# One pool for all raw tiles, tied places for the rest of the rows, and score steps and transposes at other places, in a hybrid decoder layer

## The chip, the cores and the metric

The kernel runs on one core of one Trainium2 chip. The metric is the device time of one execution in microseconds. The kernel before takes 1724.84 us, the median of three runs (1724.03 to 1726.55). The execution that the profiler recorded took 1727.64 us.

## The reference

One layer on 4096 rows of 1024 float32 values:

```python
proj = x @ w_in                      # 1024 x 2832, cut into q_a, k_a, v_a, g_a | q_b, k_b, v_b, g_b, r_b
q_a, k_a = partial_rope(q_a), partial_rope(k_a)          # 8 query heads, 2 key heads of 64, first 16 dims
out_a = softmax(window 128, with a sink per head)(q_a, k_a) @ v_a * silu(g_a)
log_a = log_sigmoid(r_b @ w_up + b_gate) / 16
o_b   = gla_chunked(q_b / 8, k_b, v_b, log_a)            # 4 heads, chunks of 64, a state carried over the chunks
out_b = o_b * rsqrt(mean(o_b ** 2) + 1e-5) * norm_w * silu(g_b)
out   = layer_norm(2 ** 0.25 * x + concat(out_a, out_b) @ w_out, ln_g, ln_b)
```

## The kernel before

The rows are worked in 32 blocks of 128 (`NB` = 32). There are three stages, each a loop over all blocks: A is the windowed attention, B the gated linear attention, C the output projection with the layer norm. A and B leave their branch in HBM (`mixd`), and C loads it again.

Every large product is made of three float32r products: a tensor is cut into a high part (a cast) and a low part (the tensor less its high part), and high x high, high x low and low x high are added up. So each loaded ("raw") tile of 128x512 float32 is cast once and subtracted once. For the rows of a block these are two tiles, q = 0 (k = 0 to 3) and q = 1 (k = 4 to 7). GpSimd casts them (L103) and VectorE subtracts (L106). Both parts go to `xq`, which has four places in stage A; the rows of block n+2 take the place of block n-2. For weights, ScalarE casts and VectorE or GpSimd subtracts.

Block n of stage A is issued in this order (L488 to L537):

- The rows of block n+2 are fetched (`fetch_x`, two DMAs on SyncE's queue).
- The query projection `pq` runs over k = 0 to 7 with three matmuls of 512 columns for each k. After every second k one step of the generator `a_scores` of block n-1 is taken. The four steps make the scores `psc` of two heads each. The first two belong to head group g = 0, the other two to g = 1. After each, VectorE masks the scores and takes the maximum. After steps two and four come ScalarE's exponentials and VectorE's normalisation (`pr`, L414).
- `pkv`, the key and value projection, follows; VectorE applies the rotation (L315 to L320).
- `pg`, the gate projection, is done "turned" for the pair of blocks (n, n+1 for even n), 6 matmuls of 256 columns for each k; an even n makes columns 0 and 1 of the pair, an odd n columns 2 and 3. So the places of a pair of rows come free in the odd block: k = 0 to 3 first, k = 4 to 7 at the end of its `pg`.
- Between parts of `pg` run the steps of `a_out` of block n-1: `turn(0)` and `turn(1)` (transposes `pt`, cut into `hl` by ScalarE and VectorE, then four masked copies `p` each by GpSimd's affine select, L439), `mul(0)` and `mul(1)` (four matmuls `po` each, L454, and VectorE's `att`). Then there are the transposes of the keys (`a_turn_k`) and of the queries (`a_turn_q`: `tq`, cut into `qs`, VectorE's parts at L351 for heads 0 to 3 of the first half and L353 for the second).
- Last come the gate (`a_gate`, VectorE's part `sg` at L364) and the generator of this block's scores.

Blocks 0 and 30 project the queries of two blocks, and blocks 1 and 31 of none.

The order on each engine is not exactly this. A planner places each instruction by its own estimate of when its inputs and buffers are ready, and prefers what is earlier in the program. Work whose inputs and buffers are free early is moved ahead, across blocks too. On the chip each engine and each DMA queue then works strictly in the planned order. `after(ins, earlier)` adds an edge that only fixes the order.

Raw tiles lie in these pools before: `xw` (two buffers) for rows in A and B and for `mixd` tiles in C; `wr` (three buffers in A, another three in B and C) for weights loaded after the start. Weights of B are loaded in A's blocks 2, 30 and 31, those of C in B's last block.

Of the kernel before, what the change touches and what calls it, by code (L numbers as in the profile page):

```python
# [9 lines left out]
F32 = mybir.dt.float32  # L10
F32R = mybir.dt.float32r
# [3 lines left out]
ALU = mybir.AluOpType  # L15
# [4 lines left out]
P = 128  # L20
# [30 lines left out]
def layer_kernel(  # L51
# [18 lines left out]
    NB = xt.shape[0]  # L70
# [4 lines left out]
    xp = ctx.enter_context(tc.tile_pool(name="xp", bufs=1))  # L75
    xw = ctx.enter_context(tc.tile_pool(name="xw", bufs=2))
    ps = ctx.enter_context(tc.tile_pool(name="ps", bufs=2, space=PSUM))
# [37 lines left out]

    def load_group(wr, src, c0, n, slot, width, early=False):
        hs, ls = [], []
        for k in range(NK):
            raw = wr.tile([P, 512], F32, tag="wraw", name=f"wraw{slot}_{k}")
            sp.dma_start(raw[:, :n], src[k, :, c0 : c0 + n])  # L120
            h = wp.tile([P, width], F32R, tag=f"wh{slot}_{k}", name=f"wh{slot}_{k}")
            l = wp.tile([P, width], F32R, tag=f"wl{slot}_{k}", name=f"wl{slot}_{k}")
            split(h[:, :n], l[:, :n], raw[:, :n], act, dve if early or k % 2 == 0 else pool)
            hs.append(h)
            ls.append(l)
        return hs, ls

    def load_halves(wr, src, c0, slot):

        hs, ls = ([wp.tile([P, 512], F32R, tag=f"w{t}{slot}_{k}", name=f"w{t}{slot}_{k}") for k in range(NK)] for t in "hl")  # L130
        for i in range(2):
            c = slice(256 * i, 256 * i + 256)
            for k in range(0, NK, 2):
                raw = wr.tile([P, 512], F32, tag="wraw", name=f"wraw{slot}_{k}_{i}")
# [26 lines left out]
    def load_x(n, heng, leng, places):  # L161
        for x in split_x(n, fetch_x(n), heng, leng, places):
            pass
        return x

# [22 lines left out]
    with ExitStack() as pa:  # L188
        e1 = pa.enter_context(tc.tile_pool(name="e1", bufs=1))
        wr = pa.enter_context(tc.tile_pool(name="wra", bufs=3))  # L190
        with ExitStack() as pstart:
# [11 lines left out]
            raws, xs = [], []  # L203
# [93 lines left out]
        vvs = {-1: v0}  # L297
        tanh = [None]

# [39 lines left out]
        def a_turn_q(n, qk):  # L339

            tq = bank("tp", f"tq{n}")
            for j in range(4):
                pe.transpose(
                    tq[:, j * P : (j + 1) * P],
                    qk[:, 2 * j : 2 * j + 2, :].rearrange("p h d -> p (h d)"),
                    ident,
                )
            qs = e1.tile([P, 8, P], F32R, tag="qs", name=f"qs{n}")
            tqv = tq.rearrange("p (j s) -> p j s", j=4)
            act.copy(qs[:64, :4, :], tqv[:64])  # L350
            dve.tensor_tensor(qs[64:, :4, :], tqv[:64], qs[:64, :4, :], ALU.subtract)  # L351
            act.copy(qs[:64, 4:, :], tqv[64:])
            dve.tensor_tensor(qs[64:, 4:, :], tqv[64:], qs[:64, 4:, :], ALU.subtract)  # L353
            return qs
# [63 lines left out]
        def a_out(n, pn):  # L418
# [4 lines left out]
            parts = {}  # L423

            def turn(g):
# [7 lines left out]
                act.copy(hr, ptv)  # L433
                dve.tensor_tensor(hl[:, 1].bitcast(F32R), ptv, hr, ALU.subtract)
                for i in range(2):
# [51 lines left out]
        for n in range(NB):  # L487
            last = n == NB - 1  # L488
            raws = fetch_x(n + 2) if 0 < n < NB - 2 else None
            both = n in (0, NB - 2)  # L490
            group = [n, n + 1] if both else [] if n in (1, NB - 1) else [n]
            pqs = [bank("pj", f"pq{m}") for m in group]
            for i in range(4):
                for m, pq in zip(group, pqs):
                    project(pq, xs[m], wq, 512, 2 * i, 2 * i + 2)
                if scores:
                    pn = next(scores)
            for m, pq in zip(group, pqs):
                qks[m] = a_q(m, pq)
            if n == NB - 2:  # L500
                wb["v"] = load_group(wr, w_b, 528, 512, 0, 512)
            for m in group:
# [3 lines left out]
            if n == 0:  # L506
                wg = load_halves(wr, w_a, 768, 2)
                raws = fetch_x(2)
            if n == NB - 2:
                wb["q"] = load_group(wr, w_b, 0, 272, 1, 272)  # L510
            if n == 2:
                wb["k"] = load_group(wr, w_b, 272, 256, 3, 256)
# [12 lines left out]
            project_turned(pg, xpair, wg, cols, 6, 7)  # L525
            qs = a_turn_q(n, qks[n])
            xs.extend(parts)
            project_turned(pg, xpair, wg, cols, 7, 8)
            next(po, None)
            if last:  # L530
                bx_next = load_x(0, pool, dve, 2)
                wb["g"] = load_group(wr, w_b, 1040, 512, 2, 512)
            a_gate(n, pg)
# [15 lines left out]
    with ExitStack() as pb:  # L549
        wr = pb.enter_context(tc.tile_pool(name="wrb", bufs=3))  # L550
        f1 = pb.enter_context(tc.tile_pool(name="f1", bufs=1))
# [230 lines left out]
        for n in range(NB):  # L782
            x, last = bx_next, n == NB - 1
            if not last:
                bx_next = load_x(n + 1, pool, dve, 2)
            pq = bank("pj", f"bq{n}")
# [19 lines left out]
            if last:  # L806
                wo[0] = load_group(wr, w_o, 0, 512, 0, 512)
            pk = bank("pj", f"bk{n}")
# [11 lines left out]
            if last:  # L820
                wo[1] = load_group(wr, w_o, 512, 512, 2, 512)
        b_attn(NB - 1)
# [6 lines left out]
    with ExitStack() as pcx:  # L829
# [126 lines left out]
```

## Time and profile before

| | us |
|---|---|
| median of 3 runs | 1724.84 |
| profiled execution | 1727.64 |
| its span, first to last instruction | 1725.9 |
| stage A, about | 0 to 672 |
| stage B, about | 672 to 1372 |
| stage C, about | 1372 to the end |

The span covers all but 1.74 us of the profiled execution. In the rows below a time in front of a line is the start from the span's beginning, the number behind it the duration, and a bracket at the end is idle time of that engine before the instruction with what ended it. Matmuls overlap their neighbours in these rows: one of 512 columns is shown some 0.39 us long and the next starts 0.23 us after it; one of 256 columns is shown 0.28 us long and the next starts 0.12 us after it. A row of a stretch gives its limits, its length, the busy us (and the number of instructions) of PE, PEld, DVE, ACT and POOL, the mean granted clock of TensorE, the busy share of the DMA engines, and GB/s.

### The profile page before, as it was taken

What the parts mean: (1) busy time and instruction counts of PE and PEld (TensorE: products, weight loads), DVE (VectorE), ACT (ScalarE), POOL (GpSimd) and SP (SyncE); (2) the same over time, 40 slices, a digit from 0 to 9 for tenths busy, and PEclk for the clock granted to TensorE, in tenths of its full rate; (3) what the DMA queues carried; (4) which work ended last, traced back from release to release, by engine and by line L of the source; (5) the groups of instructions that cost most, each with busy time, mean ns of one, the idle gap of its engine ahead of it and who ended that gap; (6) DMA issues with size and microseconds to landing.
All of it is one profiled execution on the core that took longest, in us unless ns stands there. A gap on an engine that the chain in (4) does not pass through costs nothing.

```text
span 1725.9 us, 27803 instructions
## 1 busy us (share of the span) xinstructions
PE 1684.8 (98%) x10117; PEld 1482.6 (86%) x10117; DVE 1130.8 (66%) x2602; ACT 785.4 (46%) x2110; POOL 504.6 (29%) x623
## 2 busy tenths in 40 slices
PE   8999999999999999999999999999999899999998
PEld 8788888888888887888888888888888788888886
DVE  7777777777777776666666666666666755555554
ACT  6544434444443455555555555555555622222221
POOL 1433333233333345222222222222222422222221
PEclk9999999999999999999999999999999999999999
DMA  6211111111111132111111111111111544444442
GB/s 189 83 37 43 43 41 49 42 37 38 38 38 44 37 100 80 33 38 39 39 40 38 38 38 38 38 38 38 37 38 38 172 158 143 143 143 146 147 135 86
DMA packets 76478, 119.80 MB, mean 69 GB/s; under 512 B 23858, under 2 KB 30388, under 8 KB 76340
## 3 DMA queue, kind: packets, MB, share of 16 engines
q1 hardware_dynamic: 76340, 118.02, 21.4%
q8 instruction: 80, 1.31, 0.3%
q14 instruction: 58, 0.48, 0.1%
HBM read 84.37 MB, written 33.62 MB: 68 GB/s over the span
## 4 chain that ended last, share of the span: by engine, by line
PE 83%; DVE 8%; POOL 3%; issue 3%; ACT 3%; DMA 1%; DVEq 0%; POOLq 0%; ACTq 0%; SPq 0%
PE py L173 7%; PE py L172 7%; PE py L171 7%; PE bv L173 3%; PE bg L171 3%; PE bv L172 3%; PE bv L171 3%; PE bg L173 3%; PE bg L172 3%; PE pg L185 3%; PE pg L183 3%; PE pg L184 3%; PE po L454 2%; PE psc L389 2%; PE pq L173 2%
## 5 line engine op out<-in xcount | busy, mean ns | idle before, releaser
L439 POOL TENSOR_SCALAR_AFFINE_SELECT p<-hl 128x512 fp32r<-128x512 f32 x256 | 170.3, 698 | 335.0 <-ACT hl L433 302.0
L103 POOL TENSOR_SCALAR xq<-xraw 128x512 fp32r<-128x512 f32 x124 | 77.8, 632 | 429.9 <-issue 303.1
L171 PE MATMUL py<-wh,xq 128*128 128x512 f32 x512 | 200.2, 391 | 0.0
L173 PE MATMUL py<-wh,xq 128*128 128x512 f32 x512 | 200.2, 391 | 0.0
L172 PE MATMUL py<-wl,xq 128*128 128x512 f32 x512 | 200.0, 391 | 0.0
L408 ACT ACTIVATE pr<-psc,ngm 128x128 f32<-128x128 f32 x256 | 90.7, 367 | 158.7 <-DVE ngm L403 147.1
L183 PE MATMUL pg<-xq,wh 128*128 128x256 f32 x512 | 154.7, 302 | 3.0 <-DVE vv L325 1.7
L871 POOL TENSOR_TENSOR y<-y,lg 128x1024 f32<-128x1024 f32 x31 | 74.1, 2392 | 267.2 <-ACT y L870 267.2
L185 PE MATMUL pg<-xq,wl 128*128 128x256 f32 x512 | 145.5, 284 | 0.3 <-DVE wl L106 0.3
L184 PE MATMUL pg<-xq,wh 128*128 128x256 f32 x512 | 145.2, 284 | 0.0
L106 DVE TENSOR_TENSOR xq<-xraw,xq 128x512 fp32r<-128x512 f32 (+1 forms) x132 | 111.4, 844 | 45.2 <-POOL xq L103 40.8
L172 PEld LDWEIGHTS py<-wl,xq 128*128 128x128 f32 x512 | 96.7, 189 | 20.2
L171 PEld LDWEIGHTS py<-wh,xq 128*128 128x128 f32 x512 | 96.7, 189 | 20.0
L173 PEld LDWEIGHTS py<-wh,xq 128*128 128x128 f32 x512 | 96.5, 189 | 19.9
L171 PE MATMUL bg<-wh,xq 128*128 128x512 f32 x256 | 106.2, 415 | 0.0
L101 ACT CAST xq<-mr 128x512 fp32r<-128x512 f32 x64 | 39.6, 622 | 140.2 <-PE py L172 135.1
L171 PE MATMUL bv<-wh,xq 128*128 128x512 f32 x256 | 103.2, 403 | 0.0
L171 PE MATMUL pq<-wh,xq 128*128 128x512 f32 x256 | 100.1, 392 | 1.6 <-DVE sg L364 1.6
L854 DVE SCALAR_TENSOR_TENSOR y<-xr,py 128x512 f32<-128x512 f32 x64 | 44.0, 687 | 87.8 <-PE py L173 87.7
L183 PEld LDWEIGHTS pg<-xq,wh 128*128 128x128 f32 x512 | 98.3, 192 | 3.5 <-DVE vv L325 1.9
L173 PE MATMUL pq<-wh,xq 128*128 128x512 f32 x256 | 101.1, 395 | 0.0
L172 PE MATMUL pq<-wl,xq 128*128 128x512 f32 x256 | 100.8, 394 | 0.0
(220 smaller groups left out, 5027.2 us busy)
## 6 DMA issues: line engine op xcount, KB each, us to landing
xraw<-in_xt_dram SPq DMA_DIRECT2D x124, 256.0 KB, 2.7
mr<-mx SPq DMA_DIRECT2D x64, 256.0 KB, 3.0
xr<-in_xn_dram SPq DMA_DIRECT2D x32, 512.0 KB, 3.6
out_dram<-y SPq DMA_DIRECT2D x31, 512.0 KB, 2.6
mx<-att SPq DMA_DIRECT2D x32, 256.0 KB, 2.7
mx<-mb SPq DMA_DIRECT2D x32, 256.0 KB, 2.0
wraw<-in_w_b_dram SPq DMA_DIRECT2D x16, 256.0 KB, 3.0
wraw<-in_w_o_dram SPq DMA_DIRECT2D x16, 256.0 KB, 3.2
```

The costliest lines, as they stand in the source:

```text
L103: pool.tensor_scalar(hdst, src, 1.0, 1.0, ALU.mult, ALU.mult)
L106: leng.tensor_tensor(ldst, src, hdst, ALU.subtract)
L171: pe.matmul(dst[:, :n], a, hs[k][:, :n], start=(k == 0), stop=False)
L172: pe.matmul(dst[:, :n], a, ls[k][:, :n], start=False, stop=False)
L173: pe.matmul(dst[:, :n], b, hs[k][:, :n], start=False, stop=(k == NK - 1))
L183: pe.matmul(o, hs[k][:, c], a, start=(k == 0 and i == 0), stop=False)
L184: pe.matmul(o, hs[k][:, c], b, start=False, stop=False)
L185: pe.matmul(o, ls[k][:, c], a, start=False, stop=(k == NK - 1 and i == 1))
L408: act.activation(pr[:, i], sc[i], AF.Exp, bias=ngm[:, h : h + 1], scale=0.125, accum_out=den[:, h : h + 1])
L439: pool.affine_select(o, hl[:, i], [[0, 4], [sg_, P]], ALU.is_gt if b else ALU.is_ge, 0.0, base=0, channel_multiplier=-sg_,)
L854: dve.scalar_tensor_tensor(y[:, s], xr[:, s], ALPHA, py, ALU.mult, ALU.add)
L871: pool.tensor_tensor(y, y, lg, ALU.mult)
```

## The change

All raw tiles (rows, weights, and the tiles of C) come from one pool `xw` with six buffers under one tag; the pools `wr` are gone. `fetch_x` with GpSimd issues a row tile's cast right behind its load. The subtraction (`rest_x`) is a call of its own. In stage A the subtraction of q = 0 is tied behind the last `hl` subtraction on VectorE and that of q = 1 behind the last `qs` subtraction (L353); in the order of the program the casts stand at the head of the block. The four score steps stand after k = 3, 5, 7 and 8 of `pq` (before: 2, 4, 6, 8). `turn(0)` stands after the first k of `pg` (before: ahead of it); `turn(1)` and all later steps keep their places. In stage B `load_x` does cast, cast, subtract, subtract (before: cast, subtract, cast, subtract).

```diff
-    xw = ctx.enter_context(tc.tile_pool(name="xw", bufs=2))
+    xw = ctx.enter_context(tc.tile_pool(name="xw", bufs=6))
...
-            raw = wr.tile([P, 512], F32, tag="wraw", name=f"wraw{slot}_{k}")
+            raw = xw.tile([P, 512], F32, tag="raw", name=f"wraw{slot}_{k}")
...
-    def fetch_x(n):
+    def fetch_x(n, heng, places=4):
+
         raws = []
         for q in range(2):
-            raws.append(xw.tile([P, 4, P], F32, tag="xraw", name=f"xraw{n}_{q}"))
-            sp.dma_start(raws[q], xt[n][:, 4 * q : 4 * q + 4])
+            s = slice(4 * q, 4 * q + 4)
+            raws.append(xw.tile([P, 512], F32, tag="raw", name=f"xraw{n}_{q}").rearrange("p (k s) -> p k s", k=4))
+            sp.dma_start(raws[q], xt[n][:, s])
+            if heng is pool:
+                pool.tensor_scalar(rows_of(n, places)[0][:, s], raws[q], 1.0, 1.0, ALU.mult, ALU.mult)
         return raws
 
-    def split_x(n, raws, heng, leng, places=4):
+    def rest_x(n, raws, q, places=4):
+
         h, l = rows_of(n, places)
+        s = slice(4 * q, 4 * q + 4)
+        return dve.tensor_tensor(l[:, s], raws[q], h[:, s], ALU.subtract)
+
+    def load_x(n, places):
+        raws = fetch_x(n, pool, places)
         for q in range(2):
-            s = slice(4 * q, 4 * q + 4)
-            split(h[:, s], l[:, s], raws[q], heng, leng)
-            yield h, l
...
+            rest_x(n, raws, q, places)
+        return rows_of(n, places)
...
-            raws = fetch_x(n + 2) if 0 < n < NB - 2 else None
+            raws = fetch_x(n + 2, pool) if 0 < n < NB - 2 else None
...
-                    project(pq, xs[m], wq, 512, 2 * i, 2 * i + 2)
+                    project(pq, xs[m], wq, 512, (0, 3, 5, 7)[i], (3, 5, 7, 8)[i])
...
-            next(po, None)
-            parts = split_x(n + 2, raws, pool, dve) if raws else iter(())
...
-            project_turned(pg, xpair, wg, cols, 0, 3)
+            project_turned(pg, xpair, wg, cols, 0, 1)
+            next(po, None)
+            project_turned(pg, xpair, wg, cols, 1, 3)
             next(po, None)
             project_turned(pg, xpair, wg, cols, 3, 6)
             next(po, None)
-            next(parts, None)
+            if raws:
+                ins = rest_x(n + 2, raws, 0)
+                if n > 0:
+                    after(ins.ins, hl_last[0].ins)
             a_turn_k(n, kks[n])
             project_turned(pg, xpair, wg, cols, 6, 7)
             qs = a_turn_q(n, qks[n])
-            xs.extend(parts)
+            if raws:
+                after(rest_x(n + 2, raws, 1).ins, qs_last[0].ins)
+                xs.append(rows_of(n + 2))
             project_turned(pg, xpair, wg, cols, 7, 8)
...
-                raws.append(xw.tile([P, 4, P], F32, tag="xraw", name=f"mr{n}_{q}"))
+                raws.append(xw.tile([P, 512], F32, tag="raw", name=f"mr{n}_{q}").rearrange("p (k s) -> p k s", k=4))
```

## Rows read from the trace of the kernel before

**Rows 1.** The page's busy times by engine.

```profile
PE 1684.8 (98%) x10117; PEld 1482.6 (86%) x10117; DVE 1130.8 (66%) x2602; ACT 785.4 (46%) x2110; POOL 504.6 (29%) x623
```

**Rows 2.** TensorE's waits, 81 to 616 us: total, times, longest.

```profile
PE psc L389 <- DVE qs L351: 11.1, 13, 1.4
PE pt L429 <- DVE es L404: 1.6, 7, 0.3
```

**Rows 3.** Busy times by stretch: block 5, block 6 of A; then most of B.

```profile
112.63:132.00 19.37, 19.37 (x135) 17.95 (x134) 13.61 (x33) 8.57 (x29) 6.32 (x10) 1.00 0.08 28
132.00:152.78 20.78, 19.95 (x135) 17.84 (x134) 15.93 (x38) 8.43 (x30) 6.63 (x11) 1.00 0.16 52
...
721.00:1340.00 619.00, 619.00 (x3862) 550.33 (x3861) 385.86 (x896) 342.75 (x840) 168.76 (x200) 1.00 0.13 38
```

**Rows 4.** TensorE's timeline: starts of blocks 4 and 29, and block 5's end.

```profile
91.81 0.39 PE L171 MATMUL pq<-wh,xq 128*128 128x512 f32 x1
...
125.48 0.60 PE L429 MATMUL pt<-cs,pr 128*128 128x128 f32 x4
...
128.07 1.09 PE L454 MATMUL po<-p,vv 128*128 128x512 f32 x4
...
131.08 1.09 PE L454 MATMUL po<-p,vv 128*128 128x512 f32 x4
...
134.31 0.74 PE L389 MATMUL psc<-kd,qs 128*128 128x256 f32 x4 [0.76 <-DVE qs L351]
...
596.17 0.39 PE L171 MATMUL pq<-wh,xq 128*128 128x512 f32 x1
```

**Rows 5.** VectorE's timeline in blocks 5 and 6.

```profile
123.61 0.69 DVE L414 TENSOR_TENSOR pr<-pr,rec 128x512 f32<-128x512 f32 x1
...
125.87 0.68 DVE L434 TENSOR_TENSOR hl<-pt,hl 128x512 fp32r<-128x512 f32 x1
...
128.47 0.69 DVE L106 TENSOR_TENSOR xq<-xraw,xq 128x512 fp32r<-128x512 f32 x1 [0.99 <-POOL xq L103]
129.86 0.68 DVE L463 TENSOR_TENSOR att<-po,tmp 64x512 f32<-64x512 f32 x1 [0.70 <-ACT tmp L462]
...
132.46 1.08 DVE L106 TENSOR_TENSOR xq<-xraw,xq 128x512 fp32r<-128x512 f32 x1 [1.58 <-POOL xq L103]
133.57 0.69 DVE L351 TENSOR_TENSOR qs<-tq,qs 64x512 fp32r<-64x512 f32 x1
```

**Rows 6.** GpSimd's timeline in block 5.

```profile
126.62 1.23 POOL L439 TENSOR_SCALAR_AFFINE_SELECT p<-hl 128x512 fp32r<-128x512 f32 x2 [0.91 <-DVE hl L434]
127.82 0.62 POOL L103 TENSOR_SCALAR xq<-xraw 128x512 fp32r<-128x512 f32 x1
128.59 1.07 POOL L439 TENSOR_SCALAR_AFFINE_SELECT p<-hl 128x512 fp32r<-128x512 f32 x1 [0.16 <-PE po L454]
...
131.80 1.20 POOL L103 TENSOR_SCALAR xq<-xraw 128x512 fp32r<-128x512 f32 x2 [0.38 <-DMA xraw<-in_xt_dram]
```

**Rows 7.** The start: TensorE's and GpSimd's timelines, then one stretch of 5 us.

```profile
49.18 0.63 PE L429 MATMUL pt<-cs,pr 128*128 128x128 f32 x4 [1.76 <-DVE pr L414]
...
46.67 1.83 POOL L103 TENSOR_SCALAR xq<-xraw 128x512 fp32r<-128x512 f32 x2 [4.24 <-DMA xraw<-in_xt_dram]
...
50.00:55.00 5.00, 4.15 (x14) 3.17 (x14) 3.51 (x7) 1.70 (x4) 5.00 (x8) 0.66 0.31 83
```

**Rows 8.** From A to B: TensorE's and VectorE's timelines, then one stretch.

```profile
618.67 0.50 PE L171 MATMUL pq<-wh,xq 128*128 128x512 f32 x1 [1.58 <-DVE sg L364]
...
616.09 1.08 DVE L106 TENSOR_TENSOR xq<-xraw,xq 128x512 fp32r<-128x512 f32 x1 [1.69 <-POOL xq L103]
...
665.00:670.00 5.00, 5.00 (x18) 4.20 (x18) 2.02 (x4) 2.42 (x5) 2.91 (x5) 0.55 0.18 50
```

**Rows 9.** From B to C: TensorE's timeline, then one stretch.

```profile
1368.16 0.66 PE L742 MATMUL bo<-bvv,al 128*128 128x128 f32 x4 [1.58 <-DVE al L106]
...
1370.00:1375.00 5.00, 4.61 (x14) 3.71 (x14) 2.74 (x7) 1.99 (x4) 2.36 (x3) 0.50 0.85 284
```

More of the change, by code (lines that the diff above doesn't have):

```diff
@@ L114, in load_chunk, with load_group @@
         return h, l, raw
-    def load_group(wr, src, c0, n, slot, width, early=False):
+    def load_group(src, c0, n, slot, width, early=False):
         hs, ls = [], []
         for k in range(NK):
-            raw = wr.tile([P, 512], F32, tag="wraw", name=f"wraw{slot}_{k}")
+            raw = xw.tile([P, 512], F32, tag="raw", name=f"wraw{slot}_{k}")
             sp.dma_start(raw[:, :n], src[k, :, c0 : c0 + n])
@@ L126, in load_group, with load_halves @@
         return hs, ls
-    def load_halves(wr, src, c0, slot):
+    def load_halves(src, c0, slot):
         hs, ls = ([wp.tile([P, 512], F32R, tag=f"w{t}{slot}_{k}", name=f"w{t}{slot}_{k}") for k in range(NK)] for t in "hl")
@@ L133, in load_halves @@
             for k in range(0, NK, 2):
-                raw = wr.tile([P, 512], F32, tag="wraw", name=f"wraw{slot}_{k}_{i}")
+                raw = xw.tile([P, 512], F32, tag="raw", name=f"wraw{slot}_{k}_{i}")
                 for j in range(2):
@@ L145, in rows_of @@
         return xq[:, n % places, 0], xq[:, n % places, 1]
-    def fetch_x(n):
+    def fetch_x(n, heng, places=4):
         raws = []
         for q in range(2):
-            raws.append(xw.tile([P, 4, P], F32, tag="xraw", name=f"xraw{n}_{q}"))
-            sp.dma_start(raws[q], xt[n][:, 4 * q : 4 * q + 4])
+            s = slice(4 * q, 4 * q + 4)
[3 more added lines that the diff above has]
+                pool.tensor_scalar(rows_of(n, places)[0][:, s], raws[q], 1.0, 1.0, ALU.mult, ALU.mult)
         return raws
-    def split_x(n, raws, heng, leng, places=4):
+    def rest_x(n, raws, q, places=4):
         h, l = rows_of(n, places)
+        s = slice(4 * q, 4 * q + 4)
+        return dve.tensor_tensor(l[:, s], raws[q], h[:, s], ALU.subtract)
+    def load_x(n, places):
+        raws = fetch_x(n, pool, places)
         for q in range(2):
-            s = slice(4 * q, 4 * q + 4)
-            split(h[:, s], l[:, s], raws[q], heng, leng)
-            yield h, l
[L161 to L164, printed above, removed]
+            rest_x(n, raws, q, places)
+        return rows_of(n, places)
     def project(dst, x, wg, n, k0=0, k1=NK):
@@ L189, in layer_kernel @@
         e1 = pa.enter_context(tc.tile_pool(name="e1", bufs=1))
-        wr = pa.enter_context(tc.tile_pool(name="wra", bufs=3))
         with ExitStack() as pstart:
@@ L297, in layer_kernel @@
         vvs = {-1: v0}
-        tanh = [None]
+        tanh, hl_last, qs_last = [None], [None], [None]
         def swapped(n):
@@ L352, in a_turn_q @@
             act.copy(qs[:64, 4:, :], tqv[64:])
-            dve.tensor_tensor(qs[64:, 4:, :], tqv[64:], qs[:64, 4:, :], ALU.subtract)
+            qs_last[0] = dve.tensor_tensor(qs[64:, 4:, :], tqv[64:], qs[:64, 4:, :], ALU.subtract)
             return qs
@@ L433, in turn @@
                 act.copy(hr, ptv)
-                dve.tensor_tensor(hl[:, 1].bitcast(F32R), ptv, hr, ALU.subtract)
+                hl_last[0] = dve.tensor_tensor(hl[:, 1].bitcast(F32R), ptv, hr, ALU.subtract)
                 for i in range(2):
@@ L500, in layer_kernel @@
             if n == NB - 2:
-                wb["v"] = load_group(wr, w_b, 528, 512, 0, 512)
+                wb["v"] = load_group(w_b, 528, 512, 0, 512)
             for m in group:
@@ L506, in layer_kernel @@
             if n == 0:
-                wg = load_halves(wr, w_a, 768, 2)
-                raws = fetch_x(2)
+                wg = load_halves(w_a, 768, 2)
+                raws = fetch_x(2, pool)
             if n == NB - 2:
-                wb["q"] = load_group(wr, w_b, 0, 272, 1, 272)
+                wb["q"] = load_group(w_b, 0, 272, 1, 272)
             if n == 2:
-                wb["k"] = load_group(wr, w_b, 272, 256, 3, 256)
+                wb["k"] = load_group(w_b, 272, 256, 3, 256)
             po = a_out(n - 1, pn) if n > 0 else iter(())
             pg = bank("pj", f"pg{n}")
-            next(po, None)
-            parts = split_x(n + 2, raws, pool, dve) if raws else iter(())
             cols = (0, 1) if n % 2 == 0 else (2, 3)
             xpair = xq[:, n // 2 % 2 * 2 : n // 2 % 2 * 2 + 2]
-            project_turned(pg, xpair, wg, cols, 0, 3)
+            project_turned(pg, xpair, wg, cols, 0, 1)
+            next(po, None)
+            project_turned(pg, xpair, wg, cols, 1, 3)
             next(po, None)
@@ L530, in layer_kernel @@
             if last:
-                bx_next = load_x(0, pool, dve, 2)
-                wb["g"] = load_group(wr, w_b, 1040, 512, 2, 512)
+                bx_next = load_x(0, 2)
+                wb["g"] = load_group(w_b, 1040, 512, 2, 512)
             a_gate(n, pg)
@@ L549, in layer_kernel @@
     with ExitStack() as pb:
-        wr = pb.enter_context(tc.tile_pool(name="wrb", bufs=3))
         f1 = pb.enter_context(tc.tile_pool(name="f1", bufs=1))
@@ L784, in layer_kernel @@
             if not last:
-                bx_next = load_x(n + 1, pool, dve, 2)
+                bx_next = load_x(n + 1, 2)
             pq = bank("pj", f"bq{n}")
@@ L806, in layer_kernel @@
             if last:
-                wo[0] = load_group(wr, w_o, 0, 512, 0, 512)
+                wo[0] = load_group(w_o, 0, 512, 0, 512)
             pk = bank("pj", f"bk{n}")
@@ L820, in layer_kernel @@
             if last:
-                wo[1] = load_group(wr, w_o, 512, 512, 2, 512)
+                wo[1] = load_group(w_o, 512, 512, 2, 512)
         b_attn(NB - 1)
```

## The prediction

> **What bounds the kernel now.** I read the page's busy times first. TensorE is busy 1684.8 us of a span of 1725.9 us, VectorE 1130.8 us [rows 1]. So TensorE sets the time and only what makes it wait can be won. Next I asked what TensorE waits for between 81 and 616 us, where stage A runs evenly: 11.1 us in 13 waits for VectorE's `qs` at the first score step, 1.6 us for `es` [rows 2]. Thirteen in 26 blocks means every second block, so I set two neighbours beside each other. Block 5 takes 19.37 us with TensorE busy throughout, block 6 takes 20.78 us, though both do the same 135 matmuls (pieces counted in the row) [rows 3]. The 1.41 us between them is more than the 0.76 us of idle time that the timeline shows before `psc` [rows 4]. The idle time is too small a measure: a matmul's shown end reaches past the start of its successor, so some 0.16 us of each wait (0.39 less 0.23) is shown as busy, and the late block has smaller delays behind the first. So I count block lengths. Block 4 starts at 91.81 us and block 29 at 596.17 us [rows 4]: 504.36 us for 13 even and 12 odd blocks. Taking 19.37 us for each odd one leaves 271.9 us, or 20.92 us for an even one. The excess is 1.55 us each and 20.1 us in all.
>
> The Trainium skill speaks of this under "Performance Expectations" in "Trainium Kernel Development and Optimization": matmul busy time is a bad metric since matmuls are pipelined, and the weight loads' busy share is a good one. The first half agrees with the 0.76 against 1.41 us. By the second half block 5 would have 1.42 us to spare too (17.95 busy of 19.37 us [rows 3]), an estimate from that page's rule; I take none of it, for nothing in block 5 waits.
>
> Why is the even block late? Its VectorE timeline [rows 5] shows the subtraction of a row tile at 132.46 us, after 1.58 us of idle time for GpSimd's cast, 1.08 us long, and right behind it, at 133.57 us, the `qs` part that the scores need. GpSimd's cast ran at 131.80 us, when the place in `xq` came free at the end of the odd block's `pg` [rows 6]. VectorE works in order, so `qs`, gate and `att` stand behind that subtraction. In stage B TensorE is busy 619.00 of 619.00 us [rows 3].
>
> **The change part by part.** *The ties.* The subtraction of q = 0 now follows the last `hl`, that of q = 1 follows L353. Neither can stand ahead of L351 with its cast late: the q = 0 cast has its place free when k = 3 of the odd block's `pg` is done. Without that subtraction `qs` (L351) can start when its inputs are there, some 2 us earlier. The subtractions themselves are not saved; q = 0 falls into VectorE's gap between the last `hl` (done about 127.5 us) and `att` (129.86 us) [rows 5], q = 1 into the wait for the first scores. If that second cover is gone, it costs what it pushes the softmax. The two bounds of one q = 1 subtraction are 0.69 and 1.08 us [rows 5].
>
> *The score steps.* The first step comes 9 instead of 6 matmuls into `pq`: 3 x 0.23 = 0.70 us later, and the second and third likewise; the fourth stays. This alone would hide 0.70 of the mean 0.85 us wait (11.1 / 13). Its price is that `pr` of g = 1 comes later. In block 5 it ends at 124.30 us and `pt` of g = 1 starts at 125.48 us [rows 4, 5]: a margin of 1.2 us, of which I see 0.7 us used. With a pushed q = 1 subtraction it could all be used; then `pt` is late by up to 0.6 us.
>
> *`turn(0)` one k later.* It moves 6 x 0.12 = 0.72 us. GpSimd's second pair of copies waits for VectorE's `hl` (125.87 us), which stands behind the rotation and not behind `pt` [rows 5, 6]. So `mul(0)` at 128.07 us should not move: the pair ends at 127.85 us, and the fourth matmul of `mul(0)` starts at 128.07 + 3 x 0.23 = 128.76 us, a margin of 0.9 us of which the later `hl` takes about 0.65.
>
> *Casts and six buffers.* Both blocks' rows can now be in SBUF when the places come free, so two q = 0 casts may go into the gap in which before one fits (127.82 to 128.59 us). In block 5 the copies for `mul(1)` end at 131.43 us (131.80 less the 0.38 us of idle), and its fourth matmul starts at 131.08 + 0.69 = 131.77 us [rows 4, 6]: margin 0.34 us. A second cast of 0.62 us costs 0 to 0.3 us. I take 0.2 us in each pair of blocks, the value nearest to these rows.
>
> *Sum for the even part.* 13 x (1.55 - 0.2) = 17.5 us won. Bounds: 20.1 us won, and 16 us lost if `pt` is late by 0.6 us in all 26 blocks and nothing is won.
>
> *The start.* At 46.67 us GpSimd waited 4.24 us for a row tile's load, which had to wait for one of two buffers; VectorE stood behind that cast and TensorE 1.76 us behind VectorE; from 50 to 55 us the granted clock was 0.66, that is, part of the stretch at the lower level, which costs 0.34 x 5 = 1.7 us [rows 7]. Six buffers load sooner, and the tie takes the subtraction out of the way; but block 2's weights now share the buffers. Half of the 3.5 us and the `turn(0)` shift give 2.5 us won; bounds 5 us won, 4 us lost (the 4.24 us again).
>
> *From A to B.* At 618.67 us TensorE waits 1.58 us, since the second query projection of block 30 needs the bank that `sg` frees, and `sg` stands behind a subtraction that waited 1.69 us [rows 8]. The subtraction moves and that projection starts 0.70 us later by itself: 1.7 us won. The weight loads that follow have four to six buffers instead of three. What is lost there to the clock (0.55 in one stretch of 5 us, so 2.2 us [rows 8]) could come back or grow: 0, bounds 3 us either way.
>
> *From B to C.* The same weights are cut by the same engines; one wait there is 1.58 us and the clock is 0.50 for 5 us [rows 9]. The first `mixd` tiles now queue for buffers behind 16 weight tiles. 0, bounds 4 us either way (1.58 and 2.5 us). In the rest of B and in C, TensorE covers all of it.
>
> Sum: 17.5 + 2.5 + 1.7 = 21.7 us. The profiled execution took 1727.64 us, which gives 1705.9 us; it lies 2.8 us above the median shown, so on the median's scale 1703.1 us. I predict 1703 us.
>
> **Rivals.**
>
> *A new wait takes half of it.* With `qs` early, the late work is GpSimd's copies for `mul(1)`, in every block now. A copy that meets a VectorE subtraction took 1.07 us at 128.59 us, others 0.62 us each [rows 6]. That is 0.45 us; with a second cast (0.62 us) 1.07 us in all, less the margin of 0.34 us: 0.7 us in 13 pairs, or 0.35 us in all 26 blocks, 9 us. Time 1712 us, 1708 to 1721. For it: the margin is small. Against it: block 5 had both, a cast and a slow copy, and lost nothing. The Trainium skill has the mechanism in "SBUF — State Buffer", "Who interferes with whom": a VectorE instruction with two SBUF inputs and a GpSimd instruction that reads SBUF lock each other out for a whole instruction. The trace agrees with 1.07 us for the copy and 1.08 us for the subtraction.
>
> *The ties don't move `qs`.* The planner puts other VectorE work ahead of L351, the two q = 0 subtractions or the gate, and only the later first step counts, its gain spent on later `pr`. Then the even blocks keep their excess: 1723 us, 1721 to 1728. Against it: L351 followed the subtraction directly and nothing else was waiting.
>
> *Slower: casts ahead of the copies.* GpSimd works in order. If the planner puts the q = 1 casts of the odd block ahead of the four copies for g = 1, these wait until `pg` ends (131.08 us), then for two casts (1.24 us) and then take 4 x 0.63 us. The last copy ends near 134.8 us and the fourth matmul of `mul(1)` starts 3 us late. Price 13 x 3 = 39 us against 21.7 us: 1742 us, 1728 to 1760. The point: ahead of one copy only, it costs 1.2 us a pair and the change is still ahead; ahead of two or more, it loses. For it: the casts stand earlier in the program now, their buffers no longer hold them back, and at the start a cast did stand ahead of copies while its load was late [rows 7]. Against it: in block 5 the planner put the cast behind the copies [rows 6].
>
> **How the numbers follow.** The forecast gets 0.60, with a range of its own of 1694 to 1713 us; half of it lost 0.18; no move of `qs` 0.10; casts ahead of copies 0.12. About 0.2% (3.4 us) can be told from no change: faster means below 1721.4 us, slower above 1728.3 us. Faster is 0.60 + 0.18 and a little of the third, less a little of the second: 0.78. The same is 0.10, mostly the third case. Slower is 0.12. The range from 1694 to 1725 us leaves out the fourth case, part of the third and the forecast's low end, some 0.2 in all.
>
> **What would show it.** Right: even blocks of 19.4 to 19.7 us as the odd ones; no wait of `psc` for `qs`; L351 directly behind its ScalarE part, the subtraction behind L353; the first `psc` 2.1 us after `pq` begins; no wait above 0.2 us at `po`. The start shows in the clock between 50 and 55 us, the seam in the wait near 618 us. Wrong: odd blocks longer than 19.4 us, `po` waiting for `p`, `pt` waiting for `pr`, or stage B or C changed in length.

## The result, and the profile after

The changed kernel takes 1707.73 us, median of 5 runs (1707.11 to 1708.66), against 1726.55 us of the kernel before on the same chip (1724.03 to 1729.78): a ratio of 0.9892, 95% interval 0.9878 to 0.9907. That is 18.8 us faster, where 1703 us with a range of 1694 to 1725 us was forecast. The profiled execution has a span of 1706.1 us, 19.8 us less than before.

Busy times hardly moved, as the page's first part shows beside [rows 1]: no engine has less to do.

```profile
PE 1682.2 (99%) x10117; PEld 1476.7 (87%) x10117; DVE 1125.3 (66%) x2602; ACT 784.2 (46%) x2110; POOL 504.1 (30%) x623
```

TensorE's waits from 600 us to the end (total, times, longest) answer to [rows 2, 8]: none is for `sg`. Between 81 and 610 us the view lists no wait at all, where before `psc` waited 13 times for `qs`.

```profile
PE po L457 <- POOL p L442: 2.5, 5, 1.0
PE pat L686 <- DVE xq L671: 2.4, 1, 2.4
PE pg L187 <- DVE vv L328: 1.4, 1, 1.4
PE pt L432 <- DVE pr L417: 1.2, 1, 1.2
```

The busy times by stretch are those of the start [rows 7], blocks 4 and 5, the step from A to B [rows 8], and the step to C [rows 9]. In most of B (721 to 1320 us) TensorE is busy 599.00 of 599.00 us, as before [rows 3].

```profile
50.00:55.00 5.00, 4.55 (x28) 3.62 (x27) 4.49 (x8) 3.19 (x8) 0.95 (x2) 1.00 0.19 52
88.34:107.85 19.51, 19.51 (x136) 17.89 (x134) 14.06 (x36) 8.00 (x29) 6.06 (x10) 1.00 0.13 42
107.85:127.87 20.02, 19.93 (x136) 17.81 (x134) 15.08 (x36) 8.96 (x30) 6.85 (x11) 1.00 0.13 40
600.00:721.00 121.00, 115.12 (x712) 99.51 (x711) 86.40 (x188) 68.55 (x186) 52.24 (x69) 1.00 0.28 82
1345.00:1350.00 5.00, 4.92 (x21) 3.69 (x21) 4.41 (x9) 3.63 (x8) 2.51 (x3) 0.72 0.86 322
```

The even blocks are now 19.50 us long, 1.4 us less than the mean of before; but the odd ones, 19.37 us before, are now 20.02 us, and nearly all of that counts as busy. TensorE's timeline shows where (start, length, engine, line, tile): of block 5 its beginning, the first scores 2.09 us later, `mul(0)` in 1.20 us and `mul(1)` in 1.60 us, both 1.09 us before [rows 4]; then the start of block 29.

```profile
88.34 0.39 PE L175 MATMUL pq<-wh,xq 128*128 128x512 f32 x1
...
107.85 0.39 PE L175 MATMUL pq<-wh,xq 128*128 128x512 f32 x1
...
109.94 0.63 PE L392 MATMUL psc<-kd,qs 128*128 128x256 f32 x4
...
123.31 1.20 PE L457 MATMUL po<-p,vv 128*128 128x512 f32 x4
...
126.43 1.60 PE L457 MATMUL po<-p,vv 128*128 128x512 f32 x4
...
582.14 0.39 PE L175 MATMUL pq<-wh,xq 128*128 128x512 f32 x1
```

VectorE's timeline shows the ties doing what they say [against rows 5]: `qs`, gate, `qs` and only then the q = 1 subtraction, with its cast long there; the q = 0 subtraction comes behind the last `hl`.

```profile
107.02 0.68 DVE L354 TENSOR_TENSOR qs<-tq,qs 64x512 fp32r<-64x512 f32 x1 [0.30 <-ACT qs L353]
107.75 0.69 DVE L367 SCALAR_TENSOR_TENSOR sg<-sg,pg 128x512 f32<-128x512 f32 x1
108.47 0.69 DVE L356 TENSOR_TENSOR qs<-tq,qs 64x512 fp32r<-64x512 f32 x1
109.20 0.69 DVE L162 TENSOR_TENSOR xq<-xraw,xq 128x512 fp32r<-128x512 f32 x1
...
121.53 1.28 DVE L437 TENSOR_TENSOR hl<-pt,hl 128x512 fp32r<-128x512 f32 x2
122.72 0.73 DVE L162 TENSOR_TENSOR xq<-xraw,xq 128x512 fp32r<-128x512 f32 x1
```

GpSimd's timeline of the same block [against rows 6] has the new trouble: both q = 0 casts stand ahead of the four copies for `mul(1)`, and the pair of copies at 122.28 us, which ran beside the q = 0 subtraction, took 1.68 us instead of 1.23 us. From there to 127.48 us GpSimd has no gap, so what delays the pair delays the copies for `mul(1)` too.

```profile
122.28 1.68 POOL L442 TENSOR_SCALAR_AFFINE_SELECT p<-hl 128x512 fp32r<-128x512 f32 x2 [0.81 <-DVE hl L437]
123.92 1.20 POOL L155 TENSOR_SCALAR xq<-xraw 128x512 fp32r<-128x512 f32 x2
125.09 2.39 POOL L442 TENSOR_SCALAR_AFFINE_SELECT p<-hl 128x512 fp32r<-128x512 f32 x4
127.45 1.20 POOL L155 TENSOR_SCALAR xq<-xraw 128x512 fp32r<-128x512 f32 x2
```

By starts of blocks (all listed in TensorE's timeline) the 19.8 us come from: the start, block 4 at 88.34 instead of 91.81 us, 3.47 us; blocks 4 to 28, 493.80 instead of 504.36 us, 10.56 us; from the start of block 30 to the last three matmuls of `bq`, stage B's query projection, 719.69 instead of 723.05 us, 3.36 us; from there to the end, 384.8 instead of 387.3 us, 2.55 us. This sums to 19.94 us; block 29, now 0.14 us longer, takes that much back.

### The profile page after: what moved, and what is told of

It is laid out like the page before. It is cut to its first block, busy times and chain, and to the rows that moved or that the text cites. A ratio compares the mean times of both kernels' runs of the same rounds, so it can differ in the third digit from the quotient of the medians.

```text
span 1706.1 us, 27762 instructions
## 1 busy us (share of the span) xinstructions
PE 1682.2 (99%) x10117; PEld 1476.7 (87%) x10117; DVE 1125.3 (66%) x2602; ACT 784.2 (46%) x2110; POOL 504.1 (30%) x623
## 3 DMA queue, kind: packets, MB, share of 16 engines
q1 hardware_dynamic: 76340, 118.02, 21.7%
## 4 chain that ended last, share of the span: by engine, by line
PE 60%; DVE 1%; POOL 1%; ACT 0%; issue 0%; DMA 0%; DVEq 0%; POOLq 0%; ACTq 0%
PE py L177 7%; PE py L176 7%; PE py L175 7%; PE bv L177 3%; PE bv L176 3%; PE bv L175 3%; PE bg L175 3%; PE bg L177 3%; PE bg L176 3%; PE bk L176 2%; PE bk L175 2%; PE bk L177 2%; PE bq L175 2%; PE bq L176 2%; PE bq L177 2%; PE bo L746 1%
## 5 line engine op out<-in xcount | busy, mean ns | idle before, releaser
L176 PEld LDWEIGHTS py<-wl,xq 128*128 128x128 f32 x512 | 96.4, 188 | 19.8
L162 DVE TENSOR_TENSOR xq<-xraw,xq 128x512 fp32r<-128x512 f32 x124 | 104.5, 843 | 7.8 <-POOL xq L155 3.5
L175 PE MATMUL bv<-wh,xq 128*128 128x512 f32 x256 | 103.2, 403 | 0.0
L177 PE MATMUL pq<-wh,xq 128*128 128x512 f32 x256 | 101.5, 396 | 0.0
L177 PE MATMUL bv<-wh,xq 128*128 128x512 f32 x256 | 100.7, 394 | 0.0
L176 PE MATMUL bv<-wl,xq 128*128 128x512 f32 x256 | 100.5, 393 | 0.0
```

What stands on the lines that cost most here:

```text
L162: return dve.tensor_tensor(l[:, s], raws[q], h[:, s], ALU.subtract)
L175: pe.matmul(dst[:, :n], a, hs[k][:, :n], start=(k == 0), stop=False)
L176: pe.matmul(dst[:, :n], a, ls[k][:, :n], start=False, stop=False)
L177: pe.matmul(dst[:, :n], b, hs[k][:, :n], start=False, stop=(k == NK - 1))
```

## The experiments

The theory: the ties win the even block's excess, and the 0.65 us by which odd blocks grew are the two casts ahead of `mul(1)`'s copies. Its rival: the later score steps won it, and the ties are little but order.

**Score steps alone**, in the kernel before:

```diff
-                    project(pq, xs[m], wq, 512, 2 * i, 2 * i + 2)
+                    project(pq, xs[m], wq, 512, (0, 3, 5, 7)[i], (3, 5, 7, 8)[i])
```

> The kernel before with one edit: the score steps stand after k = 3, 5, 7 and 8 of pq. Theory (VectorE's subtraction with a late cast stands ahead of qs; the first step's move hides only 0.70 us of each wait): even blocks fall from 20.9 to 20.2 to 20.4 us, odd blocks stay at 19.37 us, 7 to 9 us won in all, near 1718 us. Rival A (the steps' places are the whole gain, since another place also makes the planner order VectorE anew): even blocks near 19.4 us, 18 us won or more, 1708 us. Rival B (a later first step only delays pr): no gain, 1724 us or above.

Slower: 1727.78 against 1720.12 us, ratio 1.0041 (1.0026 to 1.0056). Odd blocks 19.63, even ones 20.83 us. The wait for `qs` is gone, but TensorE waits a step later instead (waits of the whole run):

```profile
PE pt L429 <- DVE es L404: 15.3, 13, 1.5
```

VectorE's timeline of block 4 says why: the subtraction of 1.09 us behind a late cast is still there, and the gate and the masks (L397), without which there is no softmax, come behind it.

```profile
90.84 1.09 DVE L106 TENSOR_TENSOR xq<-xraw,xq 128x512 fp32r<-128x512 f32 x1 [1.63 <-POOL xq L103]
91.85 0.67 DVE L364 SCALAR_TENSOR_TENSOR sg<-sg,pg 128x512 f32<-128x512 f32 x1
...
95.75 0.43 DVE L397 COPY_PREDICATED psc<-upt,psc 128x256 f32<-128x256 uint32 x1
```

So rival A falls, and so does my claim that the later step alone hides 0.70 us of each wait; rival B, no gain, is what happened. Here a delay of VectorE's whole queue was not hidden by moving one of its consumers.

**The changed kernel without the ties:**

```diff
-                ins = rest_x(n + 2, raws, 0)
-                if n > 0:
-                    after(ins.ins, hl_last[0].ins)
+                rest_x(n + 2, raws, 0)
...
-                after(rest_x(n + 2, raws, 1).ins, qs_last[0].ins)
+                rest_x(n + 2, raws, 1)
```

> The changed kernel without its two ties: the subtractions go where the planner puts them. Theory (the ties keep the subtractions off qs): the wait of psc for qs comes back, even blocks near 20.9 us less the 0.70 us of the later step, so about 20.2 us, and the total 5 to 10 us above the changed kernel, 1713 to 1718 us. Rival A (six buffers make the casts early enough that no subtraction is late): blocks as in the changed kernel, 19.50 and 20.02 us, total within 2 us of 1707.7 us.

1720.55 against 1720.12 us, ratio 1.0001 (0.9992 to 1.0010): all of the gain is gone, more than the 5 to 10 us that I had expected. Odd blocks are 20.45, even ones 20.16 us. VectorE's timeline at the end of a block has both subtractions around the gate and ahead of the masks (L400), the first again 1.09 us long behind a cast:

```profile
88.10 1.09 DVE L162 TENSOR_TENSOR xq<-xraw,xq 128x512 fp32r<-128x512 f32 x1 [0.65 <-POOL xq L155]
89.11 0.68 DVE L367 SCALAR_TENSOR_TENSOR sg<-sg,pg 128x512 f32<-128x512 f32 x1
...
91.27 0.69 DVE L162 TENSOR_TENSOR xq<-xraw,xq 128x512 fp32r<-128x512 f32 x1
92.59 0.43 DVE L400 COPY_PREDICATED psc<-upt,psc 128x256 f32<-128x256 uint32 x1
```

But the wait of `psc` for `qs`, which I expected back, is not there. In the even blocks `pt` waits for `pr` instead (first line, waits from 81 to 590 us), since the masks are late. In the odd ones the casts stand ahead of the copies for `mul(1)`, these take 3.29 us, and `mul(1)` takes 2.15 us (second line, TensorE's timeline of block 5):

```profile
PE pt L432 <- DVE pr L417: 5.4, 13, 0.4
126.48 2.15 PE L457 MATMUL po<-p,vv 128*128 128x512 f32 x4
```

So in this kernel the ties are needed, but not for `qs` alone: they keep the subtractions off the masks and off the copies.

**The casts tied too**, each behind the last copy that stands ahead of it in the program:

```diff
-                pool.tensor_scalar(rows_of(n, places)[0][:, s], raws[q], 1.0, 1.0, ALU.mult, ALU.mult)
+                cast = pool.tensor_scalar(rows_of(n, places)[0][:, s], raws[q], 1.0, 1.0, ALU.mult, ALU.mult)
+                if places == 4 and p_last[0] is not None:
+                    after(cast.ins, p_last[0].ins)
...
-                        pool.affine_select(
+                        p_last[0] = pool.affine_select(
```

> The changed kernel, and each cast of a row tile in stage A also tied behind the last masked copy (affine select) that stands ahead of it in the program. Theory (the 0.52 us by which odd blocks are longer than even ones comes from two casts ahead of the copies for mul(1)): odd blocks fall from 20.02 to 19.50 us, 13 x 0.52 = 6.8 us less, near 1701 us. Rival (the odd blocks' 0.52 us is the two subtractions or the ports): odd blocks stay at 20.0 us, 1707.7 us.

1699.40 against 1720.12 us, ratio 0.9877 (0.9863 to 0.9892). Every block is 19.50 us; here an odd one:

```profile
106.22:125.72 19.50, 19.50 (x135) 17.89 (x134) 14.55 (x36) 8.48 (x30) 6.44 (x11) 1.00 0.12 41
```

With the casts out of the copies' way the odd blocks' 0.52 us are gone.

**The old pools** (two buffers for rows, three for weights, each with a tag of its own), the rest of the change kept:

```diff
-    xw = ctx.enter_context(tc.tile_pool(name="xw", bufs=6))
+    xw = ctx.enter_context(tc.tile_pool(name="xw", bufs=2))
...
-            raw = xw.tile([P, 512], F32, tag="raw", name=f"wraw{slot}_{k}")
+            raw = wr[0].tile([P, 512], F32, tag="wraw", name=f"wraw{slot}_{k}")
```

> The changed kernel with the pools of before: two buffers for row tiles and mixd tiles, three of their own for weights in A and three in B and C; ties, steps and turn(0) as changed. Theory (the gain of the even blocks needs no buffers; two buffers keep the second cast out of the gap; the gain at the start and the seams is the buffers'): odd and even blocks both 19.5 us, which is 6.8 us won, and 3 to 8 us lost at the start and the two seams: 1703 to 1712 us. Rival (buffers are what frees qs, since the rows cannot be cast early with two): even blocks above 20.5 us and 1718 us or more.

1703.92 against 1720.12 us, ratio 0.9909 (0.9892 to 0.9925); again 19.50 us in every block but one (19.98 us). With two buffers the casts are planned behind the copies by themselves. From the last `bq` to the end it takes 386.5 us, 1.7 us more than with six buffers: that is what these give at the step to C, and they take 6 us in A. At the start and from A to B, where I had expected a loss too, there is none to speak of: block 4 starts at 88.01 us, and block 30 to the last `bq` takes 719.9 us.

What remained were 0.13 us in every block above 19.37. I suspected noise between chips, the score steps and `turn(0)`, and tried each, with the **changed kernel again**, unaltered, on the same chip.

> The changed kernel again, as the anchor of the runs beside it on one chip. Both theories: odd blocks 20.02 us, even blocks 19.50 us, a ratio to the kernel before between 0.987 and 0.991.

1707.50 against 1722.65 us, ratio 0.9911 (0.9894 to 0.9927); blocks of 20.04 and 19.48 us as before.

**The old score steps** in the changed kernel:

```diff
-                    project(pq, xs[m], wq, 512, (0, 3, 5, 7)[i], (3, 5, 7, 8)[i])
+                    project(pq, xs[m], wq, 512, 2 * i, 2 * i + 2)
```

> The changed kernel with the score steps back behind k = 2, 4, 6 and 8. Theory (with the ties qs is ready some 2.2 us before the first step, so the later place hides nothing more): no wait of psc for qs, blocks 20.02 and 19.50 us, total within 2 us of the changed kernel. Rival (the later steps are needed beside the ties): psc waits for qs or the masks come late, blocks 0.3 us longer or more, 8 us or more in all.

1703.06 against 1722.65 us, ratio 0.9885 (0.9870 to 0.9900). The first stretch below is block 4, the second block 5:

```profile
87.35:106.70 19.35, 19.35 (x135) 17.95 (x134) 14.16 (x36) 8.14 (x29) 5.66 (x10) 1.00 0.11 42
106.70:126.60 19.90, 19.81 (x135) 17.87 (x134) 15.67 (x36) 9.07 (x30) 6.80 (x11) 1.00 0.11 40
```

Each block becomes 0.13 to 0.15 us shorter, so with the ties the later steps cost something instead of nothing. In GpSimd's timeline of block 5 the pair of copies takes 1.23 us again, and it is the casts that meet the subtraction:

```profile
121.02 1.23 POOL L442 TENSOR_SCALAR_AFFINE_SELECT p<-hl 128x512 fp32r<-128x512 f32 x2 [0.76 <-DVE hl L437]
122.22 1.64 POOL L155 TENSOR_SCALAR xq<-xraw 128x512 fp32r<-128x512 f32 x2
123.81 2.40 POOL L442 TENSOR_SCALAR_AFFINE_SELECT p<-hl 128x512 fp32r<-128x512 f32 x4
```

And TensorE's timeline there has `mul(0)` back at 1.09 us and `mul(1)` at 1.62 us:

```profile
122.13 1.09 PE L457 MATMUL po<-p,vv 128*128 128x512 f32 x4
...
125.14 1.62 PE L457 MATMUL po<-p,vv 128*128 128x512 f32 x4
```

VectorE's timeline tells the two cases apart. Here the subtraction (next fence) starts 0.66 us behind the copies, so the second copy (0.62 us each) has begun; the subtraction is held up, and then the first cast. In the changed kernel it starts 0.44 us behind them (122.72 against 122.28 us) and the second copy is held up, which `mul(0)` waits for.

```profile
121.68 1.11 DVE L162 TENSOR_TENSOR xq<-xraw,xq 128x512 fp32r<-128x512 f32 x1
```

I had allowed the steps 2 us in all; they cost 4.4 us. Which engine holds up which is read here from starts and lengths; no run shows it by itself.

**`turn(0)` back at its old place** in the changed kernel:

```diff
-            project_turned(pg, xpair, wg, cols, 0, 1)
             next(po, None)
-            project_turned(pg, xpair, wg, cols, 1, 3)
+            project_turned(pg, xpair, wg, cols, 0, 3)
```

> The changed kernel with turn(0) back ahead of pg. Theory (the 0.13 us by which all blocks exceed 19.37 us is the second pair of copies of turn(0), slowed from 1.23 to 1.68 us by the q = 0 subtraction that runs beside it, so that mul(0) ends 0.1 us late): blocks stay at 19.50 and 20.02 us, total within 2 us of the changed kernel. Rival (the 0.13 us is the price of a second break in pg): blocks 19.37 and 19.89 us, 3.5 us less.

1713.06 against 1722.65 us, ratio 0.9942 (0.9927 to 0.9957): 5.6 us slower than the changed kernel beside it, where I expected no difference. Both kinds of block are 0.2 us longer. In GpSimd's timeline of block 4 the first pair of copies is now the slow one, and the second starts at 102.95 us, where it was 102.77 us in the changed kernel:

```profile
100.17 1.62 POOL L442 TENSOR_SCALAR_AFFINE_SELECT p<-hl 128x512 fp32r<-128x512 f32 x2 [11.06 <-ACT hl L436]
102.95 4.03 POOL L442 TENSOR_SCALAR_AFFINE_SELECT p<-hl 128x512 fp32r<-128x512 f32 x6 [1.16 <-DVE hl L437]
```

`mul(0)` takes 1.40 us there instead of 1.20 us. So beside the later steps the move of `turn(0)` is worth 0.2 us in a block.

**The q = 0 subtraction later**, behind `att` of `mul(0)`, with the casts tied:

```diff
-                dve.tensor_tensor(att[m], po[m], tmp[m], ALU.add)
+                att_last[0] = dve.tensor_tensor(att[m], po[m], tmp[m], ALU.add)
...
-                    after(ins.ins, hl_last[0].ins)
+                    after(ins.ins, att_last[0].ins)
```

> As the kernel with the casts tied, and the subtraction of q = 0 tied behind VectorE's att of mul(0) instead of the last hl, so that it no longer runs beside the copies for mul(0). Theory: all blocks 19.37 us, 0.13 x 26 = 3.4 us less than with the casts tied alone, so 10 us less than the changed kernel. Rival (a second break in pg, or the copies are not what is late): blocks stay at 19.50 us. If the subtraction now pushes qs or the masks too far: blocks above 19.5 us with psc or pt waiting.

1698.84 against 1722.65 us, ratio 0.9859 (0.9844 to 0.9874). Blocks of 19.42 us (a few 19.6 to 20.0) instead of 19.50 us, and the pair of copies in 1.23 us beside the later steps (GpSimd's timeline, block 4):

```profile
100.04 1.23 POOL L446 TENSOR_SCALAR_AFFINE_SELECT p<-hl 128x512 fp32r<-128x512 f32 x2 [0.81 <-DVE hl L441]
101.58 3.06 POOL L446 TENSOR_SCALAR_AFFINE_SELECT p<-hl 128x512 fp32r<-128x512 f32 x4 [0.32 <-PE po L461]
```

So 0.08 of the 0.13 us went with this meeting. I had expected 19.37 us; the last 0.05 us went only with the old steps, and what makes them was not traced.

**The rows' part alone** (casts issued behind their loads, and the two ties; below "the ties alone"): old pools, steps and `turn(0)`, that is, the edits of the three kernels above that put these back, together.

> The kernel before with the rows' part alone: cast behind the load, subtractions split off and tied; old pools, old score steps, turn(0) ahead of pg. Theory (the order on VectorE and GpSimd is the whole steady gain): all blocks from 19.35 to 19.40 us, 20 us won in 13 pairs of blocks, 2 to 4 us more at the start and from A to B, nothing from B to C; a ratio near 0.987. Rival (the other parts carry it together): blocks at 19.7 us or more, or psc waiting for qs, a ratio of 0.992 or more.

1702.66 against 1718.73 us, ratio 0.9897 (0.9880 to 0.9914). Blocks 4 and 5:

```profile
88.62:107.99 19.37, 19.37 (x136) 17.95 (x134) 15.44 (x36) 8.53 (x30) 6.45 (x10) 1.00 0.12 42
107.99:127.35 19.36, 19.36 (x135) 17.95 (x134) 15.29 (x36) 8.47 (x30) 6.35 (x11) 1.00 0.12 41
```

All 20 us that the forecast saw in blocks 4 to 28 come with this part, and of the start 1.7 to 3.2 us (block 4 at 88.62 us, 90.32 and 91.81 us in the two traces of the kernel before). No run has the ties with the casts at their old place in the program, so the two are not told apart. The step from A to B is as before, 723.1 us, with its wait for `sg` (waits of the whole run), and the ratio falls short of the 0.987 expected:

```profile
PE pq L177 <- DVE sg L370: 1.8, 1, 1.8
```

**The ties, the six buffers and the casts tied, with the old steps**: the edits of the casts-tied and of the old-steps kernel together.

> The changed kernel with the casts also tied behind the masked copies and the score steps back behind k = 2, 4, 6 and 8. Theory (the two costs of the change add: 0.52 us in odd blocks from casts ahead of copies, 0.14 us in each block from the later steps): all blocks 19.35 us, 10 to 11 us less than the changed kernel, a ratio to the kernel before near 0.984, the fastest of all. Rival (the two are one cost seen twice): blocks 19.50 us, as with the casts tied alone.

1695.26 against 1718.73 us, ratio 0.9856 (0.9840 to 0.9873). This is the fastest: 12 us under the changed kernel's 1707.5 (9 us by the two ratios, since these were different chips), and the interval lies below that of the changed kernel run again. Block 4 in the view by stretch, and block 5 is the same:

```profile
86.11:105.47 19.36, 19.36 (x135) 17.94 (x134) 15.14 (x36) 8.58 (x30) 6.02 (x11) 1.00 0.13 42
```

GpSimd's timeline of block 5 has the copies first:

```profile
119.80 1.22 POOL L446 TENSOR_SCALAR_AFFINE_SELECT p<-hl 128x512 fp32r<-128x512 f32 x2 [0.76 <-DVE hl L441]
121.42 2.40 POOL L446 TENSOR_SCALAR_AFFINE_SELECT p<-hl 128x512 fp32r<-128x512 f32 x4 [0.40 <-PE po L461]
123.79 1.20 POOL L157 TENSOR_SCALAR xq<-xraw 128x512 fp32r<-128x512 f32 x2
```

**The same with the old `turn(0)`** (the edit of the old-turn kernel added):

> As e10, and turn(0) back ahead of pg. Theory (turn(0) one k later is worth 0.2 us a block only beside the later steps, which make pr late for it): all blocks 19.35 to 19.40 us, total within 2 us of e10. Rival (the later turn(0) pays by itself): blocks 0.2 us longer, 5 us more.

1696.18 against 1718.73 us, ratio 0.9860 (0.9845 to 0.9875); all blocks 19.37 us. Without the later steps the place of `turn(0)` makes no difference. This kernel differs from the ties alone only in the six buffers and the tied casts, and is 6.5 us faster on the same chip: nothing of that lies in blocks 4 to 28 (484.16 against 484.21 us), all of it at the start and the two steps.

**The kernel before again**, for its trace on another chip:

> The kernel before, unchanged, for its profile on the chip of these runs. Both theories: odd blocks 19.37 us, even blocks 20.7 to 21.5 us; if this chip is faster with it than the first one, as the runs beside the other kernels say, the difference is in the even blocks and the seams, where loads and casts are waited for.

1723.0 us in one run, 1718.73 us the median of those beside it. The even blocks vary from 20.33 to 21.49 us (20.7 to 21.5 expected), and blocks 4 to 28 take 501.57 us here against 504.36 us. `psc` waits 9.6 us for `qs`, in 13 waits again, and from 600 to 721 us the granted clock is 0.97.

## Why the prediction came out

**The ties: right.** `qs` was late because a subtraction with a late cast stood ahead of it, and the rows' part undoes that: 20.1 us of excess were read from the block lengths, and the ties alone won 504.36 - 484.21 = 20.2 us over the same blocks. With the ties left out of the whole change, nothing was won. That the idle time before `psc` (11.1 us) is too small a measure was right too.

Why the cast was late was read wrongly. The prediction has it wait for its place at the end of `pg`; but the last matmul of that `pg` starts at 130.96 us, and the bracket of the cast at 131.80 us names the row tile's load [rows 6]. SyncE issued that load at 129.19 us, when the subtraction of 128.47 us had freed one of the two buffers [rows 5]. The forecast didn't suffer, since the order and not the lateness counted: with the ties alone casts wait 133.7 us for loads between 81 and 600 us (48.3 us before, 81 to 616 us), and the blocks still take 19.37 us.

**The two casts: order right, size wrong.** Odd blocks lost 0.52 us, 6.2 us in 12 of them, where 0.2 us was taken out of a bound of 0 to 0.3. The tied casts show that without them ahead of the copies this loss goes. But they need not have made it alone: 0.45 us of the delay on GpSimd is the slowed pair just ahead of them. With a pair of 1.23 us the copies for `mul(1)` would have ended near 127.03 us instead of 127.48 us, ahead of 127.12 us (126.43 + 0.69), where the fourth matmul of an undelayed `mul(1)` starts. By this estimate the casts by themselves cost no more than the 0.2 us, and what the term left out is the meeting. No run has the casts ahead without a meeting, so the split stays open. It is the rival that I gave 0.18, with its slowed copies ahead of the casts and not behind them.

**Later score steps and the subtraction in the gap: wrong.** "The subtractions themselves are not saved; q = 0 falls into VectorE's gap" held for VectorE, which was idle there, but GpSimd was not: the subtraction met the copies for `mul(0)`. The margin of 0.9 us for `mul(0)` was worked out with copies of 1.23 us; they took 1.68 us. Price 0.13 us in each of 25 blocks, 3.3 us, of which the later subtraction won back 0.08 us a block and the old steps all. That `pr` uses 0.7 of the 1.2 us before `pt` was right: `pt` doesn't wait in blocks 4 to 29, and in block 5 `pr` ends 0.50 us before it starts, by VectorE's timeline and then TensorE's:

```profile
119.54 0.68 DVE L417 TENSOR_TENSOR pr<-pr,rec 128x512 f32<-128x512 f32 x1
```

```profile
120.72 0.60 PE L432 MATMUL pt<-cs,pr 128*128 128x128 f32 x4
```

Together: 20.1 - 6.2 - 3.3 = 10.6 us, as measured (the terms are read from the same block lengths, so this is bookkeeping and no test), against 17.5 us forecast and 8.5 us by the first rival. In stage A the truth lay nearer to that rival. Its sign, that `po` would be seen waiting for `p`, did not appear as a wait between 81 and 610 us: the 0.51 us stand in `mul(1)`'s length. The sign "odd blocks longer than 19.4 us" did.

**The start, 2.5 us: mis-sized.** It gave 3.5 us. From 50 to 55 us the granted clock is now 1.00, which is the 1.7 us read there [rows 7]. "Six buffers load sooner" was not what won it: with the old pools and the rest of the change block 4 starts at 88.01 us, with the ties alone at 88.62 us. With six buffers, ties, tied casts and the old steps it starts at 86.11 us.

**From A to B, 1.7 us: mis-sized, and for another reason.** It gave 3.4 us. The wait for `sg` did go, but not by "the subtraction moves" alone: with the ties alone it is 1.8 us. It is 0.6 us with the score steps alone, and gone with both (the old-pools kernel) or with the ties and the six buffers (the old-steps kernel). What was put at 0, the clock, came back: it is 1.00 now, and 0.97 before, which over 121 us is about 3.6 us:

```profile
600.00:721.00 121.00, 114.48 (x710) 99.88 (x709) 81.72 (x186) 65.26 (x187) 52.36 (x70) 0.97 0.25 75
```

The wait and the clock add up to more than 3.4 us, other waits grew (`po` for `p`: 1.1 us before, 2.5 us after, from 600 us on), and the old-turn kernel takes 719.7 us with a clock of 0.99. So the runs don't separate what each gave.

**From B to C, 0: mis-sized.** 2.5 us, within its bounds; six buffers give about 2 us (384.5 to 385.3 us in the kernels that have them, 386.5 to 387.7 us in the others). The clock in the worst 5 us is 0.72 instead of 0.50 [rows 9], but that is not the reason: the old-pools kernel has 1.00 there throughout and takes 386.5 us. Which wait the buffers shorten was not traced.

So a term too large by 6.9 us in A was mostly made up by the start and two seams, which gave 9.4 us instead of 4.2 us: the span fell by 19.8 us where 21.7 us was forecast. That the total came so close is luck: the errors were of unrelated terms and of opposite sign. The other 2.8 of the 4.7 us between 1707.7 and 1703 us are scale: the kernel before has a median 1.7 us higher here than the one shown with its profile, and the medians differ by 1.0 us less than the profiled executions. Casts ahead of the copies, the slower case, happened in its mild form: ahead of `mul(1)`'s copies, but with the places in `xq` free already, so no wait for `pg`.

## What to carry to other kernels

When a late input stalls one engine's in-order queue, look for what stands behind it in the queue and tie the late instruction behind the urgent ones; moving the consumer back by itself only moves the wait. Then see what else the earlier data set free: deeper buffers let a planner put early work ahead of urgent work on another engine, and there it needs a tie too. Try the parts of a change one by one even when the whole wins: here two parts cancelled 9.5 us of the third's gain.

## What the runs showed of the hardware

- When a VectorE subtraction met GpSimd's work, the pair on GpSimd grew by 0.44 to 0.45 us (copies 1.23 to 1.68, casts 1.20 to 1.64), the subtraction by 0.04 (0.73) or by 0.4 us (1.11), as they were staggered; or only the subtraction grew (1.08 us beside casts of 1.20 us, block 6 before). The Trainium skill, "SBUF — State Buffer", section "Who interferes with whom", has a VectorE instruction with two SBUF inputs contend with a GpSimd instruction that reads SBUF, over a shared read interface; the trace agrees with who meets, at a price below the other's whole 0.62 to 0.69 us. The meeting costs time only where the delayed one is urgent: in the ties-alone kernel the subtraction took 1.11 us in block 4 and the block still 19.37 us.
- The kernel before differs between sets of runs (medians 1726.55, 1720.12, 1722.65, 1718.73 us), the changed one hardly (1707.73 and 1707.50 us; blocks 4 to 28 in 493.80 and 493.82 us). Of the 4.6 us between its two profiled executions 2.8 us lie in blocks 4 to 28, in the even ones. Within a set of runs the kernels with the old pools spread over 2.7 to 5.8 us, the ties alone among them (4.7 us), and all those with six buffers over 1.2 to 2.3 us. So a steadier time goes with the six buffers and not with the ties; why was not tested.
- A stall of TensorE can show as length: four matmuls of 1.09 us took 1.60 us with no wait listed. Starts of blocks are the measure.
